# Four chunks of hidden products ahead of the gate matrix, half of its one-hots on DVE, and three PSUM banks with an earlier u in the chunk loop of a PEER block

## The chip, the cores and the metric

The kernel runs on one core of one Trainium2 chip. Its time is that of the device, in microseconds (us), as the median of several runs. The engines are named as in the profile: PE is TensorE, DVE is VectorE, ACT is ScalarE, POOL is GpSimd, SP is SyncE, which here only issues transfers. All arithmetic is fp32; a product of two fp32 matrices is made as three fp32r products of a high and a low half (hi·hi, hi·lo, lo·hi).

## What is computed

One decoder block on 1024 tokens of width 1024 (16 meta tokens are put ahead and dropped at the end): two convolution mixers, a residual sum, and then the PEER channel mixer, in which almost all the time goes. With `h` the residual stream:

```python
hn = rms_norm(h, norm_ffn_g)
q = (hn @ w_q).reshape(tokens, 8, 256)
s1 = einsum("thd,hnd->thn", q[..., :128], sub_keys[:, 0]); s2 = einsum(... q[..., 128:], sub_keys[:, 1])
v1, i1 = top_k(s1, 16); v2, i2 = top_k(s2, 16)
vals, pos = top_k(v1[..., :, None] + v2[..., None, :], 16)   # over the 256 pairs of each head
idx = i1[pos // 16] * 128 + i2[pos % 16]                     # 8 x 16 experts of 16384 for each token
gates = softmax(vals)
act = gelu(einsum("chkd,cd->chk", u[idx], hn))
h = h + einsum("chk,chkd->cd", act * gates, v[idx])
out = rms_norm(h, final_norm_g)
```

`u` and `v` are tables of 16384 rows of 1024 floats, 64 MB each.

## The kernel before

The 1024 tokens are 8 tiles of 128. For the first five tiles (`ND`, 640 tokens) the experts are computed **densely**: all 16384 rows of u and v pass through PE, in 128 chunks of 128 rows, and a gate matrix that is zero except at the chosen experts weighs them. For the last three tiles the chosen rows are **gathered** by 768 indirect transfers (`fetch`, 512 KB each, issued by POOL), and DVE multiplies and adds them.

Stages, in the order of the program:

1. `front`: norms, projections, convolutions, `w_q`, scores, and the top-16 searches, which run on DVE and end the stage.
2. `gate_matrix`: for each of the five tiles, in 16 steps of 8 tokens, DVE makes the one-hot `o2` of the second key (L691), DVE and ACT make the one-hot `o1` of the first key times the gate, and PE multiplies them into a 128x128 gate matrix for each token (L705, 1280 instructions); ACT copies it out of PSUM (`st`, L708), SP stores it (`g_d`). Of the eight one-hots `o1` of a step, the first six come from a comparison in bf16 on DVE (`ob`, L693) that ACT scales (L698), and the last two from DVE alone (L700).
3. `hidden_ahead`, a generator that runs beside stage 2: for the 16 chunks 5, 13, 21, ... (`AHEAD`) it makes gelu(u·hn) early, in the PE time that the gates leave, and stores it (`p_d`). It has 64 steps (16 chunks x 2 halves of the width x 2 segments of 320 tokens, 12 products of 128x320 each). `LEAD = 4` steps are taken ahead of the gates, 0.6 (`RATE`) after each step of 8 tokens, the rest after the last gate.
4. `token_experts` for the three gathered tiles (L545, L549).
5. `dense`: for each chunk `c` a half of u at a time is transposed on PE (`tr`, L733), split by ACT (`uhi`, L154) and DVE (`ulo`, L155), and multiplied into two PSUM banks `mm` (L186 to L188: 24 products a half); ACT takes the gelu out of the banks (`p`, L824), DVE weighs it (L807), ACT and DVE split it (`phi`, `plo`). An AHEAD chunk loads `p` from `p_d` instead. The chunk of v is loaded raw and split (`vhi` on ACT, `vlo` on DVE). Every four chunks (`GRP`) `down` multiplies p and v: ten PSUM banks `ms` of 12 products of 128x512 each, added into `acc` by DVE (L791). Between these stand the gather steps (`advance`; L611 and L637 on DVE). At the end `finish` norms each tile and stores it.

Each engine runs its own instructions in the order in which the program put them; a waiting instruction holds up all behind it on its engine, and a waiting transfer on SP all transfers behind it there. The raw chunks of u and of v share three slots (`raw`, 512 KB each): a chunk of u holds its slot until its second half is transposed, a chunk of v until `vlo` is made. PSUM has 8 banks, and before they are 2 for `tr`, 2 for `mm` and 4 for `ms`, in every stage.

Of the kernel before, what the change touches and what calls it, by code (L numbers as in the profile page):

```python
# [10 lines left out]
F32 = mybir.dt.float32  # L11
F32R = mybir.dt.float32r
# [6 lines left out]
PSUM = bass.MemoryType.PSUM  # L19
DRAM = bass.MemoryType.DRAM  # L20

P = 128
D = 1024
# [19 lines left out]
GB_T = 64  # L43
GB, LAG = 8, 6
AHEAD = list(range(5, NK, 8))
# [4 lines left out]
PACE = (2, 2, 2, 2, 1, 1, 1, 1, 1, 1)  # L50
LEAD = 4
HEAD = 4
# [9 lines left out]
class Block:  # L62
    def __init__(self, ctx, tc, t):
        self.ctx, self.tc, self.nc, self.t = ctx, tc, tc.nc, t
        self.n = 0
        self.last = {}
        self.const = ctx.enter_context(self.pool("const", 1))
        self.small = ctx.enter_context(self.pool("small", 2))
        self.keep = ctx.enter_context(self.pool("keep", 1))
        self.ptr = ctx.enter_context(self.pool("ptr", 2, space=PSUM))  # L70
        self.pmm = ctx.enter_context(self.pool("pmm", 2, space=PSUM))
        self.pms = ctx.enter_context(self.pool("pms", 4, space=PSUM))
        self.dram = ctx.enter_context(self.pool("dram", 1, space=DRAM))

    def pool(self, name, bufs, right=False, **kw):
        self.n += 1
        if "space" not in kw:
            kw["reuse_waits"] = "tile"
        if right:
            kw["side"] = "right"  # L80
        return self.tc.tile_pool(name=f"{name}{self.n}", bufs=bufs, **kw)

    def name(self, s):
# [7 lines left out]
    def constants(self):  # L91
# [3 lines left out]
        self.identb = self.tile(const, [P, P], BF16, "identb")  # L95
        nc.scalar.copy(self.identb, self.ident)
        self.ones = self.tile(const, [P, P], F32, "ones")
        nc.vector.memset(self.ones, 1.0 / C)
# [482 lines left out]

    def gather_constants(self):
        self.gfin = self.tile(self.ga, [P, D], F32, "gfin", bufs=1)
        self.nc.scalar.dma_start(self.gfin, self.t["final_norm_g"].rearrange("(o d) -> o d", o=1).broadcast_to([P, D]))

# [60 lines left out]
    def finish(self, ti, h):  # L646
        o = self.tile(self.ga, [P, D], F32, "row")
        self.row_norms([(o, h, P)], self.gfin, None)
        self.nc.sync.dma_start(self.t["out"][0, ti * P:(ti + 1) * P], o)
# [4 lines left out]
    def gate_matrix(self, first, routes):  # L654

        nc, V = self.nc, self.nc.vector
        W, X, B = 8, 6, GB_T
        with self.pool("gm", 2, right=True) as gm:
# [68 lines left out]
    def prep_u(self, c, q):  # L727

        if q == 0:
            self.raw = self.load("peer_u", c)  # L730
        ps = self.tile(self.ptr, [P, 4, P], F32, "tr")
        for k in range(4):
            self.nc.tensor.transpose(ps[:, k, :], self.raw[:, (4 * q + k) * P:(4 * q + k + 1) * P], self.ident)  # L733
        uT = [self.tile(self.de, [P, 4, P], F32R, "u" + s, bufs=3) for s in ("hi", "lo")]
        self.split(*uT, ps)
        return uT

# [6 lines left out]
    def hidden_ahead(self, pool):  # L744

        T = ND * P
        segs = segments(T)
        uT = self.prep_u(AHEAD[0], 0)
        for i, c in enumerate(AHEAD):
            pu = [self.tile(self.pms, [P, 512], F32, "ms")[:, :s.stop - s.start] for s in segs]  # L750
            for q in range(2):
                cur = uT
                for s, ps in zip(segs, pu):
                    self.hidden(ps, cur, q, s)
                    if q == 1:
                        p = self.tile(pool, [P, segs[0].stop], F32, "pa")[:, :s.stop - s.start]
                        self.nc.scalar.activation(p, ps, AF.Gelu_apprx_tanh)
                        self.nc.sync.dma_start(self.p_d[i, :, s], p)
                    if s is segs[0]:
                        if q == 0:  # L760
                            uT = self.prep_u(c, 1)
                        elif i + 1 < len(AHEAD):
                            uT = self.prep_u(AHEAD[i + 1], 0)
                    yield

    def dense(self, stream):
# [9 lines left out]
        with self.pool("dn", 2, right=True) as dn:  # L776
# [19 lines left out]
            main = [c for c in range(NK) if c not in AHEAD]  # L796
            uT = [self.prep_u(main[0], q) for q in range(2)]
            for c in range(NK):
# [17 lines left out]
                else:  # L816
                    main.pop(0)
                    pu = [self.tile(self.pmm, [P, 512], F32, "mm")[:, :s.stop - s.start] for s in segs]
                    for q in range(2):
                        for s, ps in zip(segs, pu):  # L820
                            self.hidden(ps, uT[q], q, s)
                            if q == 1:
# [3 lines left out]
                                advance(1)  # L826
                        if main:
                            uT[q] = self.prep_u(main[0], q)
                        if q == 0:
# [12 lines left out]
def body(tc, t):  # L842
    with ExitStack() as ctx:
# [11 lines left out]
        b.gb = ctx.enter_context(b.pool("gb", GB))  # L855
        b.gather_constants()
        b.last = {}
# [20 lines left out]
```

## Time and profile before

| | |
|---|---|
| runs | 2879.54, 2871.32, 2884.39 us; median 2879.54 |
| profiled execution | 2871.9 us, span 2870.1 us |
| busy share of the span | PE 94%, DVE 85%, ACT 33%, POOL 32% |
| chain that ended last | PE 64%, DVE 16%, ACT 9%, DMA 9%; of that raw v loads 7%, `o` on ACT (L698) 4% |
| mean TensorE clock granted | 0.987 of full |
| gate loop, first to last L705 | 679.0 to 984.7 us |
| chunk loop | 1027 to 2861 us |

The busy share of PE is an average over stages with different limits: in the top-16 part PE stands, in the gate stage ACT is as full as PE, in the chunk loop PE is fullest. The profiled execution lies 7.6 us under the median of the three runs.

### The profile page before, as it was taken

Reading aid. Unit: us, or ns where it says so; the run is one execution under the profiler, and the core shown is the slowest. Engines: PE = TensorE matmul, PEld = TensorE weight load, DVE = VectorE, ACT = ScalarE, POOL = GpSimd, SP = SyncE. Lnnn points to the kernel's source line nnn. Section 1 sums busy time; section 2 is a strip of 40 time slices with the busy share of each in tenths; the row PEclk is TensorE's granted clock in tenths of the full one; section 3 lists DMA queues with packets and bytes.
Section 4 is the critical chain, followed back from the end, with each engine's and each line's share of the span. In section 5 each row is a group of like instructions: output and inputs, shape, how many; then the busy total and the mean of one; then the engine's idle time right before and its main releaser. Section 6 shows DMA issues by size and latency. Waiting matters only on the chain.

```text
span 2870.1 us, 43789 instructions
## 1 busy us (share of the span) xinstructions
PE 2712.1 (94%) x16481; PEld 2485.9 (87%) x16481; DVE 2434.9 (85%) x5024; ACT 945.3 (33%) x1887; POOL 919.0 (32%) x793
## 2 busy tenths in 40 slices
PE   6999999986999989999999999999999999999998
PEld 6999989976888988898888889888888889888887
DVE  5998777998777569889889898889899988989986
ACT  4112431116999731222222212222222222222222
POOL 0000011110000025445544454445544544545440
PEclk9999999998999999999999999999999999999999
DMA  3112221101656789999989999999999999989992
GB/s 112 45 45 82 95 96 37 38 19 43 181 163 174 211 315 325 329 321 332 324 311 319 320 331 334 321 329 326 333 326 325 326 327 319 326 316 333 330 313 82
DMA packets 299540, 684.08 MB, mean 238 GB/s; under 512 B 20617, under 2 KB 153737, under 8 KB 299328
## 3 DMA queue, kind: packets, MB, share of 16 engines
q0 software_dynamic: 110592, 402.70, 39.4%
q1 hardware_dynamic: 188256, 276.92, 28.9%
q8 instruction: 130, 2.13, 0.3%
q10 hardware_dynamic: 480, 1.65, 0.1%
q14 instruction: 82, 0.67, 0.1%
HBM read 624.05 MB, written 57.15 MB: 237 GB/s over the span
## 4 chain that ended last, share of the span: by engine, by line
PE 64%; DVE 16%; ACT 9%; DMA 9%; issue 2%; SPq 0%; DVEq 0%; ACTq 0%
PE ms L188 12%; PE ms L187 12%; PE ms L186 12%; PE mm L188 7%; PE mm L186 7%; PE mm L187 7%; DMA raw<-in_peer_v_dram 7%; ACT o L698 4%; DVE row L637 3%; PE tr L733 2%; PE mm L705 2%; DVE vlo L155 2%; ACT st L708 2%; DVE g L611 1%; DVE s L467 1%
## 5 line engine op out<-in xcount | busy, mean ns | idle before, releaser
L588 POOL DMA_INDIRECT g<-in_peer_u_dram,ix x384 | 435.1, 1133 | 831.1 <-DVE ix L549 391.1
L186 PE MATMUL mm<-nhi,uhi 128*128 128x320 f32 x1792 | 573.1, 320 | 32.4 <-ACT p L824 32.0
L588 POOL DMA_INDIRECT g<-in_peer_v_dram,ix x384 | 440.6, 1147 | 455.1 <-DVE row L637 387.6
L188 PE MATMUL mm<-nhi,ulo 128*128 128x320 f32 x1792 | 557.7, 312 | 15.7 <-DVE ulo L155 15.1
L187 PE MATMUL mm<-nlo,uhi 128*128 128x320 f32 x1792 | 554.7, 310 | 0.0
L186 PE MATMUL ms<-vhi,phi 128*128 128x512 f32 x1280 | 501.4, 392 | 1.5 <-ACT phi L154 1.4
L188 PE MATMUL ms<-vhi,plo 128*128 128x512 f32 x1280 | 498.8, 390 | 0.0
L187 PE MATMUL ms<-vlo,phi 128*128 128x512 f32 x1280 | 498.7, 390 | 0.0
L637 DVE SCALAR_TENSOR_TENSOR row<-g,w,row 128x1024 f32<-128x1024 f32 x384 | 492.0, 1281 | 6.1 <-DMA row<-hd 4.7
L611 DVE SCALAR_TENSOR_TENSOR g<-g,row 128x1024 f32<-128x1024 f32 x384 | 464.5, 1222 | 0.0
L186 PEld LDWEIGHTS mm<-nhi,uhi 128*128 128x128 f32 x1792 | 338.4, 189 | 42.4 <-ACT p L824 40.3
L188 PEld LDWEIGHTS mm<-nhi,ulo 128*128 128x128 f32 x1792 | 337.5, 188 | 24.9 <-DVE ulo L155 23.9
L187 PEld LDWEIGHTS mm<-nlo,uhi 128*128 128x128 f32 x1792 | 338.7, 189 | 1.2
L154 ACT CAST phi<-p 128x320 fp32r<-128x320 f32 x256 | 116.4, 459 | 561.6 <-PE ms L187 340.8
L186 PEld LDWEIGHTS ms<-vhi,phi 128*128 128x128 f32 x1280 | 240.5, 188 | 51.0 <-ACT phi L154 2.4
L188 PEld LDWEIGHTS ms<-vhi,plo 128*128 128x128 f32 x1280 | 240.5, 188 | 50.6 <-DVE plo L155 0.5
L154 ACT CAST vhi<-raw 128x1024 fp32r<-128x1024 f32 x128 | 132.9, 1049 | 456.7 <-PE ms L188 316.5
L187 PEld LDWEIGHTS ms<-vlo,phi 128*128 128x128 f32 x1280 | 240.6, 188 | 49.0
L791 DVE TENSOR_TENSOR acc<-acc,ms 128x512 f32<-128x512 f32 x320 | 219.4, 685 | 34.7 <-PE ms L188 33.9
L155 DVE TENSOR_TENSOR ulo<-tr,uhi 128x512 fp32r<-128x512 f32 x256 | 175.4, 687 | 52.7 <-ACT uhi L154 51.8
L155 POOL TENSOR_TENSOR wlo<-wraw,whi 128x1024 fp32r<-128x1024 f32 x16 | 38.0, 2378 | 568.6 <-ACT whi L154 568.6
L154 ACT CAST uhi<-tr 128x512 fp32r<-128x512 f32 x256 | 149.4, 584 | 198.3 <-PE tr L733 195.9
(201 smaller groups left out, 4978.5 us busy)
## 6 DMA issues: line engine op xcount, KB each, us to landing
raw<-in_peer_u_dram SPq DMA_DIRECT2D x128, 512.0 KB
raw<-in_peer_v_dram SPq DMA_DIRECT2D x128, 512.0 KB
gd<-st SPq DMA_DIRECT2D x40, 1024.0 KB
g<-gd SPq DMA_DIRECT2D x64, 640.0 KB
wraw<-in_w_in_dram SPq DMA_DIRECT2D x20, 512.0 KB
wraw<-in_peer_w_q_dram SPq DMA_DIRECT2D x16, 512.0 KB
g<-in_peer_u_dram,ix POOLq DMA_INDIRECT x384
g<-in_peer_v_dram,ix POOLq DMA_INDIRECT x384
```

What stands on the lines that cost most here:

```text
L154: nc.scalar.copy(hi, src)
L155: self.mark(eng.tensor_tensor(lo, src, hi.bitcast(F32), op=OP.subtract))
L186: self.nc.tensor.matmul(ps, lh(a), rh(b), start=first and i == 0, stop=False)
L187: self.nc.tensor.matmul(ps, lh(a), rl(b), start=False, stop=False)
L188: last = self.nc.tensor.matmul(ps, ll(a), rh(b), start=False, stop=final and i == n - 1)
L588: self.nc.gpsimd.indirect_dma_start(out=g, out_offset=None, in_=self.t[table][0], in_offset=bass.IndirectOffsetOnAxis(ap=ix, axis=0))
L611: self.after(nc.vector.scalar_tensor_tensor(ut, ut, 1.0, b["x"], op0=OP.mult, op1=OP.mult, accum_out=b["act"][:, k:k + 1]))
L637: self.after(nc.vector.scalar_tensor_tensor(b["h"], b.pop(k), res[0][:, k:k + 1], b["h"], op0=OP.mult, op1=OP.add))
L698: nc.scalar.activation(o1[:, m, :], ob[:, :, m], AF.Copy, scale=eT[:, 2, c:c + 1])
L705: nc.tensor.matmul(pg[:, :, m], o2[:, 4 * z + m, :], o1[:, 4 * z + m, :], start=True, stop=True)
L708: nc.scalar.copy(st[:, :, c:c + 4], pg)
L791: self.mark(V.tensor_tensor(acc[:, i, dd], acc[:, i, dd], po, op=OP.add))
```

## The change

Five edits in one. (a) `LEAD` goes from 4 to 16: four AHEAD chunks ahead of the gates instead of one, so that with 48 steps beside the gates all 64 are used up and none stands behind them. (b) `X` goes from 6 to 4: of each step's eight one-hots four are made on ACT and four on DVE, and `ob` shrinks from 128x768 to 128x512. (c) In `hidden_ahead` the low half of u no longer comes from a subtraction on DVE: PE adds minus `uhi` into the bank that holds the transposes (one 128x512 product with a negative identity, L760), and ACT copies the rest out (L761). (d) `banks` makes the PSUM pools anew ahead of `dense`, with 2 banks for `tr`, 3 for `mm` and 3 for `ms`. (e) In `dense` u is transposed and split three halves ahead instead of two, with four buffers instead of three, and the raw chunk of u is loaded right after the last half of the one ahead (`early`). `finish` loads `final_norm_g` (512 KB) for each tile into a gather slot instead of keeping it.

```diff
-LEAD = 4
+LEAD = 16
...
-        W, X, B = 8, 6, GB_T
+        W, X, B = 8, 4, GB_T
...
+    def banks(self, tr, mm, ms):
+
+        if self.psum is not None:
+            self.psum.close()
+        self.psum = ExitStack()
+        mk = lambda name, bufs: self.psum.enter_context(
+            self.tc.tile_pool(name=self.name(name), bufs=bufs, space=PSUM, reuse_waits="tile"))
+        self.ptr, self.pmm, self.pms = mk("ptr", tr), mk("pmm", mm), mk("pms", ms)
...
     def finish(self, ti, h):
         o = self.tile(self.ga, [P, D], F32, "row")
-        self.row_norms([(o, h, P)], self.gfin, None)
+        g = self.tile(self.gb, [P, D], F32, "g")
+        self.nc.sync.dma_start(g, self.t["final_norm_g"].rearrange("(o d) -> o d", o=1).broadcast_to([P, D]))
+        self.row_norms([(o, h, P)], g, None)
...
     def prep_u(self, c, q):
 
         if q == 0:
-            self.raw = self.load("peer_u", c)
+            self.raw = self.early.pop(c, None) or self.load("peer_u", c)
...
+    def prep_ahead(self, c, q):
...
+        for k in range(4):
+            nc.tensor.matmul(ps[:, k, :], self.raw[:, (4 * q + k) * P:(4 * q + k + 1) * P], self.ident,
+                             is_transpose=True, start=k == 0, stop=k == 3)
+        hi, lo = (self.tile(self.de, [P, 4, P], F32R, "u" + s, bufs=4) for s in ("hi", "lo"))
+        flat = lambda x: x.rearrange("p a b -> p (a b)")
+        nc.scalar.copy(hi, ps)
+        nc.tensor.matmul(flat(ps), self.minus, flat(hi), start=False, stop=True, skip_group_check=True)
+        nc.scalar.copy(lo, ps)
+        return hi, lo
...
-            uT = [self.prep_u(main[0], q) for q in range(2)]
+            parts = [(c, q) for c in main for q in range(2)]
+            made = []
+
+            def prepare():
+
+                if parts:
+                    c, q = parts.pop(0)
+                    made.append(self.prep_u(c, q))
+                    if q == 1 and parts:
+                        self.early[parts[0][0]] = self.load("peer_u", parts[0][0])
+
+            for _ in range(3):
+                prepare()
...
                     for q in range(2):
+                        uT = made.pop(0)
                         for s, ps in zip(segs, pu):
-                            self.hidden(ps, uT[q], q, s)
+                            self.hidden(ps, uT, q, s)
...
-                        if main:
-                            uT[q] = self.prep_u(main[0], q)
+                        prepare()
...
+        b.banks(2, 3, 3)
```

How the built order moves, at three places. (The lines of the changed kernel are some ten higher: L186 to L188 are L197 to L199 there, L154 is L165, L676 is L686, L705 is L715, L724 is L734, L824 is L862.)

PE, at the point where the gates begin (L676 and L686 turn the first tile's key lists; `ms` is a bank, `n` the normed tokens). Before:

```order
L449 MATMUL ms_6564<-kT_2909,qT_6562 128x128 x3
L733 MATMUL tr_6635<-ident_75,raw_6633 128x128 x4
L733 MATMUL tr_6658<-ident_75,raw_6633 128x128 x4
L186 MATMUL ms_6644<-nhi_110,uhi_6640 128x320
L187 MATMUL ms_6644<-nlo_111,uhi_6640 128x320
L186 MATMUL ms_6645<-nhi_110,uhi_6640 128x320
L187 MATMUL ms_6645<-nlo_111,uhi_6640 128x320
L676 LDWEIGHTS oh_6426
L676 MATMUL ms_6348<-identb_80,oh_6426 128x128
```

After, the last of the rows that stand ahead of it:

```order
L197 MATMUL ms_6882<-nhi_112,uhi_6900 128x320
L198 MATMUL ms_6882<-nlo_113,uhi_6900 128x320
L760 MATMUL tr_6934<-uhi_6939,minus_82 128x512
L199 MATMUL ms_6882<-nhi_112,ulo_6901 128x320
L197 MATMUL ms_6882<-nhi_112,uhi_6900 128x320
L198 MATMUL ms_6882<-nlo_113,uhi_6900 128x320
L199 MATMUL ms_6882<-nhi_112,ulo_6901 128x320
L197 MATMUL ms_6882<-nhi_112,uhi_6900 128x320
L198 MATMUL ms_6882<-nlo_113,uhi_6900 128x320
L199 MATMUL ms_6882<-nhi_112,ulo_6901 128x320
L686 LDWEIGHTS oh_6428
L686 MATMUL ms_6350<-identb_80,oh_6428 128x128
```

Ahead of the first gate row PE has 192 products of 128x320 now (four chunks of 48), where it had 4 of the first chunk; a product on PE does not pass another, so the gates wait for all of them.

PE, behind the last gate product. Before (140 more products of 128x320 and 19 transposes follow, and then L545):

```order
L705 MATMUL mm_9984<-o_1509_9972,o_1508_9971 128x128
L705 MATMUL mm_9990<-o_1509_9972,o_1508_9971 128x128 x4
L187 MATMUL ms_10015<-nlo_111,uhi_9967 128x320
L188 MATMUL ms_10015<-nhi_110,ulo_9968 128x320
L186 MATMUL ms_10015<-nhi_110,uhi_9967 128x320
L187 MATMUL ms_10015<-nlo_111,uhi_9967 128x320
L188 MATMUL ms_10015<-nhi_110,ulo_9968 128x320
```

After:

```order
L715 MATMUL mm_10235<-o_1539_10223,o_1538_10222 128x128
L198 MATMUL ms_10097<-nlo_113,uhi_10115 128x320
L715 MATMUL mm_10241<-o_1539_10223,o_1538_10222 128x128
L199 MATMUL ms_10097<-nhi_112,ulo_10116 128x320
L715 MATMUL mm_10241<-o_1539_10223,o_1538_10222 128x128 x3
L556 LDWEIGHTS identb_80
L556 MATMUL mm_10303<-oh_10291,identb_80 128x128
```

Nothing of the 16 chunks is left there, and the rows of `token_experts` (L556, before L545) follow at once.

ACT in the chunk loop, behind the `down` of chunks 8 to 11. Chunk 13 is an AHEAD chunk, so the next chunks with products of u are 14, 15 and 16; the pairs `mm_12312`, `mm_12313` and before `mm_12257`, `mm_12258` are the banks of chunk 14, `mm_12409` and `mm_12354` the first bank of chunk 15. Raw 12403 and 12348 are v of chunk 14, raw 12500 and 12445 v of chunk 15. Before:

```order
L154 CAST vhi_12226<-raw_12228 128x1024 [waits DMAHW5_49,PE_49]
L154 CAST phi_12232<-p_12239 128x320 [waits DMAHW2_49,DVE_49]
L154 CAST vhi_12247<-raw_12249 128x1024 [waits DMAHW6_49,PE_49]
L154 CAST uhi_12290<-tr_12285 128x512 [waits PE_49]
L154 CAST vhi_12346<-raw_12348 128x1024 [waits DMAHW4_49]
L824 ACTIVATE p_12309<-mm_12257 128x320 [waits DVE_49,PE_49]
L154 CAST phi_12255<-p_12309 128x320 [waits DVE_49]
L824 ACTIVATE p_12329<-mm_12258 128x320 [waits PE_49]
L154 CAST uhi_12342<-tr_12337 128x512 [waits PE_49]
L154 CAST phi_12255<-p_12329 128x320 [waits DVE_49]
L154 CAST vhi_12443<-raw_12445 128x1024 [waits DMAHW6_49]
L154 CAST uhi_12387<-tr_12382 128x512 [waits PE_49]
```

After:

```order
L165 CAST vhi_12302<-raw_12304 128x1024 [waits DMAHW7_49,PE_49]
L165 CAST uhi_12343<-tr_12338 128x512 [waits PE_49]
L862 ACTIVATE p_12364<-mm_12312 128x320 [waits DVE_49,PE_49]
L165 CAST vhi_12401<-raw_12403 128x1024 [waits DMAHW4_49]
L165 CAST phi_12310<-p_12364 128x320 [waits DVE_49]
L862 ACTIVATE p_12384<-mm_12313 128x320 [waits PE_49]
L165 CAST uhi_12397<-tr_12392 128x512 [waits PE_49]
L165 CAST phi_12310<-p_12384 128x320 [waits DVE_49]
L165 CAST uhi_12440<-tr_12435 128x512 [waits PE_49]
L165 CAST vhi_12498<-raw_12500 128x1024 [waits DMAHW6_49]
L862 ACTIVATE p_12461<-mm_12409 128x320 [waits PE_49]
L862 ACTIVATE p_12481<-mm_12410 128x320 [waits DVE_49,PE_49]
```

The first gelu of chunk 14 now stands ahead of `vhi` of chunk 14 and no longer behind it; `vhi` of chunk 15 still stands ahead of the first gelu of chunk 15.

SP at the same place, the raw loads of v 14, u 16, v 15, u 17 before:

```order
L724 DMA raw_12348<-in_peer_v_dram 128x1024 [waits DMAHW5_49,DVE_49]
L724 DMA raw_12380<-in_peer_u_dram 128x1024 [waits DMAHW6_49,DVE_49]
L724 DMA raw_12445<-in_peer_v_dram 128x1024 [waits DMAHW1_49,PE_49]
L724 DMA raw_12479<-in_peer_u_dram 128x1024 [waits DMAHW4_49,DMAHW7_49,DVE_49,Activation_49]
L724 DMA raw_12726<-in_peer_v_dram 128x1024 [waits DMAHW6_49,DMAHW0_49,DVE_49]
```

After, u 16, v 14, u 17, v 15, u 18:

```order
L734 DMA raw_12347<-in_peer_u_dram 128x1024 [waits DMAHW5_49,DVE_49]
L734 DMA raw_12403<-in_peer_v_dram 128x1024 [waits DMAHW4_49,PE_49]
L734 DMA raw_12444<-in_peer_u_dram 128x1024 [waits DMAHW7_49,DVE_49]
L734 DMA raw_12500<-in_peer_v_dram 128x1024 [waits DMAHW6_49,DMAHW4_49,DVE_49]
L734 DMA raw_12543<-in_peer_u_dram 128x1024 [waits DMAHW3_49,PE_49]
```

A load that waits for DVE takes the slot of a v, one that waits for PE that of a u. By the addresses in the two built programs, u 16 takes the slot of v 13 before and of v 12 after; v 14 that of v 12 before, and after that of u 15, so behind the transposes of its second half; v 15 that of u 15 before, and after that of v 14. From there on the changed kernel has two slots under u and one under v: v 15, v 16, v 17, v 18, v 19 and v 20 follow each other through the same slot.

## Rows read from the trace of the kernel before

**Rows 1.** Windows: us, each engine's busy time, TensorE clock, DMA share, GB/s

```profile
700.00:950.00 250.00, 232.89 (x1739) 210.75 (x1738) 188.56 (x371) 245.66 (x595) 0.00 (x0) 0.99 0.60 170
1050.00:2800.00 1750.00, 1697.37 (x9632) 1533.33 (x9631) 1565.17 (x2294) 435.03 (x809) 867.20 (x760) 1.00 0.91 324
```

**Rows 2.** Timeline of PE ahead of the gates: start, us, instruction, [idle before <-releaser]

```profile
...
663.70 3.50 PE L676 MATMUL ms<-identb,oh 128*128 128x128 bf16 x32 [14.24 <-DVE s L467]
...
672.96 0.47 PE L186 MATMUL ms<-nhi,uhi 128*128 128x320 f32 x1
673.23 0.47 PE L187 MATMUL ms<-nlo,uhi 128*128 128x320 f32 x1
...
679.00 0.38 PE L705 MATMUL mm<-o,o 128*128 128x128 f32 x2
```

**Rows 3.** Instruction groups of the gate loop (675:985): busy, mean ns | idle before

```profile
...
L698 ACT ACTIVATE o<-ob,eT 128x128 f32<-128x128 bf16 x480 | 186.2, 470 | 2.4 <-DVE ob L693 2.2
...
L708 ACT COPY st<-mm 128x512 f32<-128x512 f32 x160 | 91.0, 583 | 3.9 <-PE mm L705 3.4
...
L700 DVE TENSOR_SCALAR o<-iota,eT 128x128 f32<-128x128 f32 x160 | 47.8, 343 | 0.0
L693 DVE TENSOR_TENSOR ob<-iob,e1b 128x768 bf16<-128x768 bf16 x80 | 42.5, 556 | 41.6 <-ACT o L698 41.4 <-ACT e1b L684 0.2
...
L155 DVE TENSOR_TENSOR ulo<-tr,uhi 128x512 fp32r<-128x512 f32 x25 | 17.2, 686 | 2.2 <-ACT uhi L154 2.1
```

**Rows 4.** Timeline of PE after the last gate product

```profile
...
985.67 0.49 PE L733 MATMUL tr<-ident,raw 128*128 128x128 f32 x3
...
1008.13 1.07 PE L545 MATMUL mm<-oh,identb 128*128 128x128 bf16 x16
```

**Rows 5.** Instruction groups of the chunks (1050:2800)

```profile
L186 PE MATMUL mm<-nhi,uhi 128*128 128x320 f32 x1712 | 547.7, 320 | 32.4 <-ACT p L824 32.0 <-issue 0.3
L188 PE MATMUL mm<-nhi,ulo 128*128 128x320 f32 x1713 | 533.1, 312 | 15.7 <-DVE ulo L155 15.1
...
L154 ACT CAST vhi<-raw 128x1024 fp32r<-128x1024 f32 x120 | 124.5, 1049 | 442.6 <-PE ms L188 316.5 <-DMA raw<-in_peer_v_dram 126.1
```

**Rows 6.** Timeline of SP after the output products of chunks 8 to 11

```profile
1210.53 0.33 SPq L724 DMA_DIRECT2D raw<-in_peer_v_dram  x1
...
1217.76 0.33 SPq L724 DMA_DIRECT2D raw<-in_peer_v_dram  x1
1219.91 0.33 SPq L724 DMA_DIRECT2D raw<-in_peer_u_dram  x1
```

**Rows 7.** Timeline of ACT there

```profile
...
1216.80 1.05 ACT L154 CAST vhi<-raw 128x1024 fp32r<-128x1024 f32 x1 [2.41 <-DMA raw<-in_peer_v_dram]
1217.75 0.43 ACT L824 ACTIVATE p<-mm 128x320 f32<-128x320 f32 x1
...
1224.87 1.05 ACT L154 CAST vhi<-raw 128x1024 fp32r<-128x1024 f32 x1 [2.59 <-DMA raw<-in_peer_v_dram]
```

**Rows 8.** Timeline of PE there

```profile
...
1213.17 0.60 PE L733 MATMUL tr<-ident,raw 128*128 128x128 f32 x4
...
1217.13 0.60 PE L733 MATMUL tr<-ident,raw 128*128 128x128 f32 x4
1218.23 0.42 PE L186 MATMUL mm<-nhi,uhi 128*128 128x320 f32 x1 [0.50 <-ACT p L824]
```

**Rows 9.** Timeline of SP after the output products of chunks 12 to 15

```profile
...
1266.19 0.33 SPq L724 DMA_DIRECT2D raw<-in_peer_v_dram  x1
...
1273.27 0.33 SPq L724 DMA_DIRECT2D raw<-in_peer_v_dram  x1
```

**Rows 10.** Timeline of ACT there

```profile
...
1270.93 1.05 ACT L154 CAST vhi<-raw 128x1024 fp32r<-128x1024 f32 x1 [1.77 <-DMA raw<-in_peer_v_dram]
...
1277.53 1.06 ACT L154 CAST vhi<-raw 128x1024 fp32r<-128x1024 f32 x1 [1.37 <-DMA raw<-in_peer_v_dram]
```

**Rows 11.** Window of a later group, just after PE had waited for ACT

```profile
...
1622.50:1625.50 3.00, 3.00 (x15) 2.96 (x14) 3.00 (x5) 1.24 (x3) 0.94 (x1) 0.54 0.76 214
```

## What was predicted

> **What bounds the kernel now.** I read the windows first, then for each stage the groups of instructions with their idle time, and at last the timelines of the places where an engine waits. In the gate stage the windows show ACT busy 245.66 of 250 us and PE 232.89, DVE 188.56 [rows 1]: both PE and ACT are nearly full, ACT the fuller. In the chunk loop PE is busy 1697.37 of 1750 us, DVE 1565.17, ACT 435.03, the DMA engines 0.91 at 324 GB/s [rows 1]: PE bounds it, with DVE and DMA close behind. What can still be taken from PE there is its idle time: 32.0 us for the gelu `p` on ACT and 15.1 us for `ulo` on DVE [rows 5], 47.1 us in all. In each case PE's bank or operand is late because ACT stands at `vhi`, which waits 126.1 us in the stretch for a raw v [rows 5]. That is the thing to follow: the gelu is cheap, but it stands in line behind a load.
>
> **The start of the gates (LEAD).** Before, PE starts on the key lists (L676) at 663.70, where it had idled 14.24 us for DVE's scores; the first gate product is at 679.00 [rows 2]. After, four chunks stand ahead on PE. A half chunk (24 products, four transposes) takes 1217.13 − 1213.17 = 3.96 us at full clock [rows 8], so four chunks take 31.7 us. They begin where that idle time does, at 663.70 − 14.24 = 649.5, but the banks for the second chunk are those of the scores, which DVE gives back at about 664 and 672, where PE goes on before [rows 2]. So about one chunk fits into the wait, and three, 23.8 us, come after 668: L686 at about 692, later by 28, less what DVE finishes meanwhile: before, 15.3 us lie between L676 and the first gate product because DVE is still at the top-16; with DVE done that shrinks to some 8. I put the first gate product at 700, 21 us later. Bounds: 15 (half of the second chunk fits too) and 28 (the clock stays at its lower level longer: at 672.96 and 673.23 products start 0.27 us apart [rows 2]).
>
> **The gate loop (LEAD, X, the low half on PE).** It takes 984.7 − 679.0 = 306 us. At the shares of [rows 1] ACT has 300 us of work in it, PE 285, DVE 230. ACT loses two of six one-hots, 160 x 186.2/480 = 62 us, and gains a copy of 583 ns for each of 22 low halves, 13 us [rows 3]: 251. DVE gains 160 one-hots at 47.8/160 = 0.30, 48 us, loses a third of `ob`, 14, and the 25 `ulo`, 17 [rows 3]: 247. PE has 44 products fewer (551 for 595 in the built order) and 22 of 128x512 more, at most 0.26 us each (3.96/24 x 512/320 [rows 8]): 285 − 7 + 6 = 284, which counts modelled ends twice at times; by the starts it is nearer 280. So PE is the bound after. ACT now is 98% full in its loop; if PE reaches the same, the loop takes 288 us, 18 less. Bounds: 0 (three engines each above 80% wait for each other in turn) and 26 (PE without a gap).
>
> **Behind the gates.** From 985.67 to 1008.13 PE does the rest of the AHEAD chunks [rows 4]. None is left: 22.5 us, no bound needed, except that L545 could find DVE's lists not ready; DVE has slack there, and I put nothing.
> Gate stage: 18 + 22.5 − 21 = about **20 us won**; bounds −5 and 33.
>
> **The chunk loop.** Three banks remove the case in which one late gelu stops PE at once, and u three halves ahead the waits for `ulo`: at most 47.1 us. Giving one bank from `ms` to `mm` I cost at nothing: DVE's addition follows 12 products of 128x512, and three banks leave PE two such spans, 2 x 12 x 0.26 = 6 us, before it needs the bank again; if DVE were later, it would be 1 to 2 us for each `down`.
> But the raw slots go the other way. In the built order two of three are under u and one under v, so the v of the next chunk is loaded only after `vlo` of the last. From the rows: a load takes 6.27 us (1210.53 to 1216.80), 7.11 (1217.76 to 1224.87) [rows 6, 7], 4.74 and 4.26 [rows 9, 10]; from `vhi`'s start to the next load that its slot lets go 3.11 (1216.80 to 1219.91) or 2.34 (1270.93 to 1273.27) [rows 6, 7, 9, 10]. One round of a v slot so takes 6.6 to 10.2 us, and PE needs one v for each 7.92 us.
> I follow it for both kinds of group, with T the end of the last `down`, 1209.65 (1213.17 less 24 products).
> (i) AHEAD group (three chunks of u, 14, 15, 16). v 14 is loaded when u 15 is transposed, T+4.3, lands T+10.5 to 11.4; v 15 at T+12.9 to 14.5, lands T+17.1 to 21.6; then 1.05 for `vhi` and 0.43 for the gelu of chunk 15, which stands behind it on ACT: T+18.6 to 23.1. PE wants that bank, with three banks, for the second segment of chunk 16, at T+15.9+1.8 = T+17.7. It waits 0.9 to 5.4 us. I take 1.6, near the low end, because the second loads of a group (4.26) come when DVE has waited and asked for fewer gathers.
> (ii) Full group (17 to 20). v 17 is loaded at T+0.9, v 18 and v 19 one round each later; the gelus are due at T+9.7, T+17.7 and T+25.7 and come at T+9.2 to 10.1, 15.8 to 20.3, 22.5 to 30.5: 0 to 4.8 us, I take 0.4.
> Before, the same two places cost 47.1 us over the 15.4 pairs of groups in the stretch, 3.1 us a pair (0.50 us in this AHEAD group [rows 8]). After, 2.0 a pair, 31 us. Won: **16 us**; bounds 33 won (0.9 a pair) and 110 lost (10.2 a pair, every load at its longest).
> `finish` now loads `final_norm_g`; the two loads inside the loop stand on SP ahead of raw loads and wait for a gather slot, of which one comes free each 1750/760 = 2.3 us [rows 1]: **2 us lost**, bounds 0 and 5. The six at the end are issued ahead of the last norms.
>
> **Sum.** 2871.9 − 20 − 16 + 2 = 2838 us, against the profiled execution (span 2870.1 and 1.8 around it). That execution lies 7.6 us under the median 2879.54; against the median the same sum is 2845. I keep 2838.
>
> **A rule that speaks against it.** Just after a PE wait in a later group the granted clock is 0.54 of full for 3 us, which is the lower level of 1.2 GHz, though the stretch as a whole has 1.00 [rows 1, 11].
> By the Trainium skill, "TensorE: Matmul & The Clock Gate", section "HAM oscillation — how this bites in real kernels", a loop that waits for a transfer on each pass falls back to the lower clock each time and pays for the restart on each pass. Were it so here, waits that stay once or twice in each of the 30 groups would cost 1.4 us more each (0.46 of 3 us), some 43 us, and the time would be 2881; the mean of 1.00 in the stretch says that the trace seldom shows it.
>
> **The rivals.**
> *One slot for v (slower).* ACT's order puts `vhi` of chunk 15, 18, 19 ahead of the gelus that free the banks. If a load takes 7 us under full DMA and `vlo` comes 3 us after, the round is 10 us against 7.92, the lag adds up through the group, and PE loses 5.4 + 4.8 us a pair. Above 5.4 us a pair (rounds of about 9 us) it eats the gate stage's gain as well: 2871.9 − 20 + 2 + 15.4 x (5.4 − 3.1) = 2889 at 5.4 + 0, past 2900 with both. For it: 7.11 and 6.27 are rows, DMA stands at 0.91. Against it: 4.26 and 4.74 are rows too, and a waiting DVE asks for fewer gathers.
> *The chunk loop stays as it is.* v's lateness takes what the banks give: 2871.9 − 20 + 2 = 2854.
> *The gate start eats the gate stage.* Start 28 us later, loop 9 shorter: 22.5 + 9 − 28 = 4 won; with 16 − 2 of the chunk loop 2854.
> *All waits go.* Loads near 4.3 us: 2871.9 − 20 − 33 + 2 = 2821, and 2808 with the gate stage at its best.
> *The restart at the lower clock after each wait*: 2881, as above.
>
> **How the numbers follow.** Forecast (gate stage and chunk loop both win, 2818 to 2850) 0.46; all waits go (2800 to 2818) 0.08; chunk loop unchanged (2850 to 2865) 0.16; gate start late 0.08; one slot for v, net loss in the loop (2865 to 2910) 0.18; restart 0.04. A measurement of this kernel can tell about 0.5%, 14 us. Faster holds the first two, most of the next two: 0.67; same 0.18; slower 0.15. The range 2800 to 2884 leaves out the worse half of the v case and the best ends; the likeliest case alone is 2818 to 2850.
>
> **What would show it.** First gate product near 700, last near 988, L545 straight after; ACT under 88% and PE near full in the loop. In the chunk loop: PE's idle for `p` under 25 us and for `ulo` under 8; raw v loads issued one `vlo` after the other; ACT's `vhi` waiting for raw v more than 126.1 us. If PE waits for `p` more than 60 us, the v slot is the cause and the forecast is wrong; if the first gate product is past 708, the start is.

## The result and the profile after

The changed kernel takes 2844.08 us (median of 4 runs, 2841.62 to 2848.59), the kernel before 2877.38 beside it: a ratio of 0.9881, 95% interval 0.986 to 0.9902, so 33 us less. Forecast were 2838 us and a gain both in the gate stage and in the chunk loop. The time came out, the sum did not: the gate stage won more than twice what was put down, and the chunk loop lost.

The profiled execution is the longest of the four, 2848.59 us, span 2846.8. Its windows, as [rows 1] (after the stretch and its length: busy us and count of PE, of PE's weight loads, of DVE, ACT and POOL, then clock, DMA share and GB/s):

```profile
700.00:950.00 250.00, 245.62 (x1949) 233.93 (x1948) 223.73 (x531) 223.04 (x547) 0.00 (x0) 1.00 0.63 180
1050.00:2800.00 1750.00, 1688.63 (x9542) 1525.63 (x9541) 1540.88 (x2258) 419.20 (x801) 878.51 (x743) 0.99 0.90 321
```

In the gate stage PE has gone from 232.89 to 245.62 of 250 us, ACT from 245.66 to 223.04, DVE from 188.56 to 223.73: PE bounds it now. In the chunk loop PE is less busy than before, 1688.63 for 1697.37. The timeline of PE, as [rows 2, 4, 8]:

```profile
691.50 1.96 PE L686 MATMUL ms<-identb,oh 128*128 128x128 bf16 x32
...
698.22 0.94 PE L715 MATMUL mm<-o,o 128*128 128x128 f32 x6
...
964.33 1.95 PE L556 MATMUL mm<-oh,identb 128*128 128x128 bf16 x32
...
1179.47 0.63 PE L743 MATMUL tr<-ident,raw 128*128 128x128 f32 x4 [1.16 <-DMA raw<-in_peer_u_dram]
...
1190.95 0.41 PE L197 MATMUL mm<-nhi,uhi 128*128 128x320 f32 x1 [1.17 <-ACT p L862]
```

L686 at 691.50 and the first gate product at 698.22 are what was forecast (692 and 700). `token_experts` begins at 964.33, where it began at 1008.13: 43.8 us earlier, against 20. From there to the end of the span it is 1882.5 us now and was 1862.0: 20.5 us given back in this execution. The groups of the gate loop (705:980), as [rows 3]:

```profile
L708 ACT ACTIVATE o<-ob,eT 128x128 f32<-128x128 bf16 x305 | 103.3, 409 | 1.9 <-PE mm L715 1.7 <-DVE ob L703 0.2
...
L718 ACT COPY st<-mm 128x512 f32<-128x512 f32 x156 | 88.7, 587 | 17.2 <-PE mm L715 16.9
L710 DVE TENSOR_SCALAR o<-iota,eT 128x128 f32<-128x128 f32 x308 | 84.3, 343 | 0.0
...
L703 DVE TENSOR_TENSOR ob<-iob,e1b 128x512 bf16<-128x512 bf16 x76 | 29.9, 421 | 0.7 <-ACT o L708 0.6
```

`ob` used to wait 41.4 us for ACT's one-hots and now waits 0.6, and it is ACT that waits for PE, 16.9 us at `st`. The groups of the chunk loop (1050:2800), as [rows 5]:

```profile
L197 PE MATMUL mm<-nhi,uhi 128*128 128x320 f32 x1688 | 543.2, 322 | 17.3 <-ACT p L862 17.0
...
L199 PE MATMUL mm<-nhi,ulo 128*128 128x320 f32 x1688 | 524.8, 311 | 0.0
...
L743 PE MATMUL tr<-ident,raw 128*128 128x128 f32 x840 | 130.1, 278 | 44.0 <-DMA raw<-in_peer_u_dram 25.8 <-DVE ulo L166 15.2 <-DVE vlo L166 2.6
L165 ACT CAST vhi<-raw 128x1024 fp32r<-128x1024 f32 x122 | 128.2, 1051 | 599.5 <-PE ms L199 302.9 <-DMA raw<-in_peer_v_dram 287.3 <-PE tr L743 8.9
```

PE's wait for the gelu fell from 32.0 to 17.0 us and that for `ulo` ahead of a product from 15.1 to nothing. But the transposes (L743), which waited 3.0 us in all before, now wait 25.8 us for a raw u and 15.2 for `ulo` to give back one of the two `tr` banks. And ACT waits 287.3 us for a raw v, where it was 126.1. SP and ACT behind the `down` of chunks 8 to 11, as [rows 6, 7]; first SP:

```profile
1172.41 0.33 SPq L734 DMA_DIRECT2D raw<-in_peer_u_dram  x1
1174.82 0.33 SPq L734 DMA_DIRECT2D raw<-in_peer_v_dram  x1
...
1184.27 0.33 SPq L734 DMA_DIRECT2D raw<-in_peer_v_dram  x1
```

then ACT:

```profile
1181.93 1.05 ACT L165 CAST vhi<-raw 128x1024 fp32r<-128x1024 f32 x1 [4.91 <-DMA raw<-in_peer_v_dram]
...
1189.52 1.04 ACT L165 CAST vhi<-raw 128x1024 fp32r<-128x1024 f32 x1 [2.34 <-DMA raw<-in_peer_v_dram]
1190.47 0.76 ACT L862 ACTIVATE p<-mm 128x320 f32<-128x320 f32 x2
```

The round of the one v slot can be read off: v 14 asked for at 1174.82, cut from 1181.93, v 15 asked for at 1184.27, cut from 1189.52, and only then, at 1190.47, the gelu of chunk 15, for which PE waits 1.17 us at 1190.95. The raw u asked for at 1172.41 lands 7 us later too, 1.16 us after PE wants it.

### The profile page after: what moved, and what is told of

Its sections match the earlier page's. It is cut to its first block, busy times and chain, and to the rows that moved or that the text cites. A ratio compares the mean times of both kernels' runs of the same rounds, so it can differ in the third digit from the quotient of the medians.

```text
span 2846.8 us, 44008 instructions
## 1 busy us (share of the span) xinstructions
PE 2707.5 (95%) x16513; PEld 2494.9 (88%) x16513; DVE 2434.5 (86%) x5152; ACT 881.6 (31%) x1762; POOL 950.9 (33%) x793
## 4 chain that ended last, share of the span: by engine, by line
PE 48%; DVE 27%; DMA 14%; issue 6%; ACT 4%; SPq 0%; ACTq 0%; DVEq 0%
DMA raw<-in_peer_v_dram 11%; PE ms L198 10%; PE ms L197 10%; PE ms L199 10%; DVE row L645 6%; DVE g L619 6%; PE mm L715 4%; PE mm L197 4%; PE mm L198 4%; PE mm L199 4%; DVE ulo L166 2%; DVE vlo L166 2%; DVE acc L817 2%; DVE p L845 1%; DVE plo L166 1%
## 5 line engine op out<-in xcount | busy, mean ns | idle before, releaser
L596 POOL DMA_INDIRECT g<-in_peer_u_dram,ix x384 | 449.3, 1170 | 790.0 <-DVE g L619 368.9
L596 POOL DMA_INDIRECT g<-in_peer_v_dram,ix x384 | 459.6, 1197 | 442.2 <-DVE row L645 366.4
L197 PE MATMUL mm<-nhi,uhi 128*128 128x320 f32 x1792 | 577.1, 322 | 18.0 <-ACT p L862 17.0
L199 PE MATMUL mm<-nhi,ulo 128*128 128x320 f32 x1792 | 557.8, 311 | 0.0
L197 PE MATMUL ms<-vhi,phi 128*128 128x512 f32 x1280 | 502.0, 392 | 0.1
L199 PE MATMUL ms<-vhi,plo 128*128 128x512 f32 x1280 | 498.8, 390 | 0.0
L197 PEld LDWEIGHTS mm<-nhi,uhi 128*128 128x128 f32 x1792 | 341.5, 191 | 26.2 <-ACT p L862 24.1
L199 PEld LDWEIGHTS mm<-nhi,ulo 128*128 128x128 f32 x1792 | 340.2, 190 | 0.0
L165 ACT CAST vhi<-raw 128x1024 fp32r<-128x1024 f32 x128 | 134.4, 1050 | 617.1 <-DMA raw<-in_peer_v_dram 304.9
L166 DVE TENSOR_TENSOR vlo<-raw,vhi 128x1024 fp32r<-128x1024 f32 x128 | 156.7, 1224 | 167.8 <-ACT vhi L165 167.6
L165 ACT CAST phi<-p 128x320 fp32r<-128x320 f32 x256 | 115.8, 460 | 594.7 <-PE ms L198 312.0
L199 PEld LDWEIGHTS ms<-vhi,plo 128*128 128x128 f32 x1280 | 240.6, 188 | 50.7
L197 PEld LDWEIGHTS ms<-vhi,phi 128*128 128x128 f32 x1280 | 240.7, 188 | 50.3 <-DVE acc L817 1.4
L743 PE MATMUL tr<-ident,raw 128*128 128x128 f32 x896 | 139.5, 280 | 53.8 <-DMA raw<-in_peer_u_dram 31.6
```

The lines of the kernel that those rows point to most:

```text
L165: nc.scalar.copy(hi, src)
L166: self.mark(eng.tensor_tensor(lo, src, hi.bitcast(F32), op=OP.subtract))
L197: self.nc.tensor.matmul(ps, lh(a), rh(b), start=first and i == 0, stop=False)
L199: last = self.nc.tensor.matmul(ps, ll(a), rh(b), start=False, stop=final and i == n - 1)
L596: self.nc.gpsimd.indirect_dma_start(out=g, out_offset=None, in_=self.t[table][0], in_offset=bass.IndirectOffsetOnAxis(ap=ix, axis=0))
```

## The experiments

Twelve kernels, in three sets, each timed beside the kernel before.

**First set: the two parts of the change, and the two parts of the chunk loop's.** `gates_alone` is the changed kernel with the chunk loop's banks and order of u put back; the other two put back one of them, and `gates_raw4` adds a slot:

```diff
             for _ in range(3):       # gates_alone, banks_two_ahead, gates_raw4: range(2)
                 prepare()
...
-                    if q == 1 and parts:          # left out in the same three
-                        self.early[parts[0][0]] = self.load("peer_u", parts[0][0])
...
-        b.banks(2, 3, 3)             # left out in gates_alone, three_ahead_alone, gates_raw4
...
-        r = self.tile(self.de, [P, D], F32, "raw", bufs=3)
+        r = self.tile(self.de, [P, D], F32, "raw", bufs=4)      # gates_raw4
```

Expected of `gates_alone`: 

> The changed kernel's edits up to the last gate stay; in the chunk loop PSUM is 2, 2, 4 banks again and u is prepared two halves ahead with its raw load in front of its own transposes, as before. Theory A (the chunk loop's part of the change loses time, because two raw slots stand under u and one under v): the first down starts as early as in the changed kernel (about 1031 us) and from there to the end it takes 1793 us as before, not 1807; about 2830 us, 14 less than the changed kernel. Theory B (the loop lost nothing by itself, and only shifted because DMA and gathers start differently): as the changed kernel, 2844.

Expected of `banks_two_ahead`: 

> The changed kernel with 2, 3, 3 banks, but u two halves ahead and no early raw load. Theory A: the third bank takes most of PE's 32.0 us of waits for the gelu away and the slots are those of before; PE waits for p under 15 us, ACT waits for raw v about 126 us as before; 2805 to 2820 us. Theory C (three ms banks or the bank order cost the time): no better than the changed kernel, 2844, with gates_alone faster than it.

Expected of `three_ahead_alone`: 

> The changed kernel with 2, 2, 4 banks in the loop, u three halves ahead and raw u loaded early. Theory A: the one slot for v makes the gelus late and two banks pass it on to PE at once; PE waits for p over 40 us, ACT for raw v near 290 us; 2860 to 2880. Theory C: faster than the changed kernel, 2830.

Expected of `gates_raw4`: 

> As gates_alone, with a fourth raw slot (and three buffers for the halves of u). Theory A: v no longer waits for a slot; ACT's wait for raw v falls from 126 us to under 50 and PE's for p from 32 to under 15; 2810 us. Theory D (a raw v is late because the DMA engines are full, not for want of a slot): the waits stay, 2830.

| kernel | median us | ratio to before (95%) |
|---|---|---|
| changed | 2844.08 | 0.9881 (0.986 to 0.9902) |
| gates_alone | 2833.41 | 0.9849 (0.9832 to 0.9865) |
| banks_two_ahead | 2842.29 | 0.9886 (0.9866 to 0.9906) |
| three_ahead_alone | 2861.64 | 0.994 (0.9921 to 0.9959) |
| gates_raw4 | 2831.96 | 0.9842 (0.9823 to 0.9862) |

Without the chunk loop's part the kernel is 10.7 us faster than with it, as theory A said. (The two intervals overlap a little, but the four runs, 2832.82 to 2834.79, all lie under the four of the changed kernel, with the kernel before at 2877 beside both.) Three halves ahead with an early load, by itself, loses 28 us. But the third bank, which by theory A should have won 10 to 25, won nothing (its four runs spread from 2832.17 to 2848.74; the trace is of the fastest, and why the others are longer was not traced). The waits say why (1050:2780; us in all, times, longest), first those of `gates_alone`:

```profile
ACT vhi L165 <- DMA raw<-in_peer_v_dram: 127.2, 56, 6.9
...
PE mm L197 <- ACT p L860: 29.1, 29, 2.8
...
PE mm L199 <- DVE ulo L166: 13.5, 20, 3.0
...
PE tr L743 <- DMA raw<-in_peer_u_dram: 3.5, 7, 0.9
```

and those of `banks_two_ahead`:

```profile
ACT vhi L165 <- DMA raw<-in_peer_v_dram: 125.3, 57, 5.9
...
PE mm L199 <- DVE ulo L166: 33.1, 37, 2.1
...
PE tr L743 <- DMA raw<-in_peer_u_dram: 9.3, 11, 1.7
...
PE mm L197 <- ACT uhi L165: 7.1, 6, 2.6
...
PE mm L197 <- ACT p L860: 1.0, 2, 0.7
```

The wait for the gelu is gone, 1.0 us, and what ACT does next after the same late `vhi`, `uhi` and with it `ulo`, is what PE waits for now: 51 us in all for 46 in `gates_alone`. The time is also the one that theory C named, but PE has no wait for the addition that frees an `ms` bank here, and `three_ahead_alone`, for which C expected 2830, took 2861.64. Beside the early u the third bank is worth something: 2861.64 without it, 2844.08 with it. With only two banks and u three halves ahead, the gelu takes it all (`three_ahead_alone`, the same window):

```profile
ACT vhi L165 <- DMA raw<-in_peer_v_dram: 253.7, 65, 8.7
...
PE mm L197 <- ACT p L862: 56.2, 36, 3.6
...
PE tr L743 <- DMA raw<-in_peer_u_dram: 17.4, 14, 2.4
```

A fourth raw slot beside the old order of u moved nothing either (`gates_raw4`, the same window):

```profile
ACT vhi L165 <- DMA raw<-in_peer_v_dram: 157.6, 44, 7.9
...
PE mm L197 <- ACT p L860: 26.9, 18, 4.9
PE mm L199 <- DVE ulo L166: 22.8, 30, 1.2
```

Theory A, as a matter of slots alone, fell here: ACT still stands at `vhi` for 157.6 us, in the order that the program's scheduler gave it. No run gave a fourth slot to the changed kernel's own order, with u three halves ahead.

**Second set: is it ACT's order, and what is X worth?** `late_cut` takes `gates_raw4`, asks for v at the same place, but cuts it one chunk later and on ACT behind that chunk's first gelu. `half_gathers` is `gates_alone` with every second gathered row left out. `gates_x6` and `gates_lead4` put one number back.

```diff
-                vh, vl = (self.tile(dn, [P, D], F32R, "v" + s, bufs=GRP) for s in ("hi", "lo"))
-                self.split(vh, vl, self.load("peer_v", c))
-                pend.append((ph, pl, vh, vl))
+                pend.append([ph, pl, self.load("peer_v", c)])     # late_cut
...
+            def cut():               # called after the next chunk's products, ahead of down
+                if pend and len(pend[-1]) == 3:
+                    raw = pend[-1].pop()
+                    vh, vl = (self.tile(dn, [P, D], F32R, "v" + s, bufs=GRP) for s in ("hi", "lo"))
+                    self.after(nc.scalar.copy(vh, raw))           # after the marked gelu
+                    self.mark(V.tensor_tensor(vl, raw, vh.bitcast(F32), op=OP.subtract))
+                    pend[-1] += [vh, vl]
...
-                                nc.scalar.activation(p, ps, AF.Gelu_apprx_tanh)
+                                ins = nc.scalar.activation(p, ps, AF.Gelu_apprx_tanh)
+                                if s is segs[0]:
+                                    self.mark(ins)
...
-        W, X, B = 8, 4, GB_T
+        W, X, B = 8, 6, GB_T         # gates_x6
-LEAD = 16
+LEAD = 4                             # gates_lead4
...
-                b[k] = self.fetch("peer_v", r[1][:, k:k + 1])
+                b[k] = self.fetch("peer_v", r[1][:, k:k + 1]) if k % 2 == 0 else b[k - 1]   # half_gathers; peer_u too
```

Expected of `late_cut`: 

> gates_alone with four raw slots, three buffers for the halves of u, and the cut of v (vhi, vlo) one chunk later and on ACT behind the next chunk's first gelu, so that no gelu stands behind a raw v that has just been asked for. Theory A (the waits of PE come from ACT standing at vhi for a late raw v): ACT's wait for raw v falls from 127 us to under 20, PE's for p, ulo and raw u from 46 in all to under 15; about 2800 us. Theory D (DVE or the DMA engines bound the loop, and a wait taken away at one place comes back at another): PE's waits only change their names; 2822 to 2835.

Expected of `half_gathers`: 

> gates_alone with every second gather left out (the gathered row before is used again, so the last three tiles come out otherwise); DVE's and POOL's other work stays. Theory A and D both say that a raw chunk lands sooner with less traffic: DMA share from 0.91 to about 0.6, landing of raw v from 6.5 us to near 3.5, ACT's wait for raw v under 40 us. If PE's waits fall under 15 us and the time to about 2800, the landing time is what the waits are made of; if PE still waits over 30 us, DVE's order is.

Expected of `gates_x6`: 

> gates_alone with six one-hots on ACT again. By the prediction's sum ACT gets 62 us of work back and bounds the loop: 266 us become about 315, 2875 to 2885 us. Rival (X was worth little, LEAD and the low half on PE did it): under 2845.

Expected of `gates_lead4`: 

> gates_alone with LEAD = 4. The first gate product comes some 19 us earlier (679), the loop stays at 266 us, and 22 us of products stand behind the last gate again: about 2836 us, a difference of 3. Rival (the wait for the scores hides most of the four chunks): 2845 to 2850.

`late_cut` takes 2779.81 us, ratio 0.9668 (0.9651 to 0.9684): 53.6 us less than `gates_alone` and 52.2 less than `gates_raw4`, which has the same slots; more than was expected. Its groups (1050:2700):

```profile
L197 PE MATMUL mm<-nhi,uhi 128*128 128x320 f32 x1680 | 534.8, 318 | 0.0
L199 PE MATMUL mm<-nhi,ulo 128*128 128x320 f32 x1680 | 519.8, 310 | 3.5 <-DVE ulo L166 3.4
...
L743 PE MATMUL tr<-ident,raw 128*128 128x128 f32 x840 | 126.4, 273 | 8.6 <-DMA raw<-in_peer_u_dram 8.3
...
L826 ACT CAST vhi<-raw 128x1024 fp32r<-128x1024 f32 x120 | 125.1, 1042 | 0.0
```

`vhi` does not wait at all, PE 12 us. On the timeline of ACT the cast now stands behind the gelu, and the raw v has landed (in 1050:2700 a cast starts a median of 34.6 us after SP asked for its v):

```profile
1169.69 0.44 ACT L868 ACTIVATE p<-mm 128x320 f32<-128x320 f32 x1 [1.17 <-PE mm L199]
1170.03 1.04 ACT L826 CAST vhi<-raw 128x1024 fp32r<-128x1024 f32 x1
```

The edit moves `vlo` on DVE with the cast; what that does by itself was not separated. Theory D, that DVE or the DMA engines would bring the waits back elsewhere, fell: both do the same work in less time (DVE is busy 1531.62 of 1650 us for 1474.42 in `gates_alone`, the DMA share is 0.93 for 0.92). `half_gathers` takes 2770.67 us (two executions), 0.9632 (0.9611 to 0.9652), with the DMA share down to 0.67:

```profile
ACT vhi L165 <- DMA raw<-in_peer_v_dram: 57.3, 53, 3.0
...
PE mm L197 <- ACT p L862: 4.3, 8, 1.1
...
PE mm L199 <- DVE ulo L166: 1.5, 1, 1.5
```

ACT still waits 57.3 us for raw v, more than the 40 expected, but PE only 5.8 in its products. From SP's issue to the cast of a raw v that ACT had to wait for it is a median of 4.6 us, and 6.4 in `gates_alone`. So the late landing is the one half of the cause, and ACT's order the other; less traffic, or the new order together with a fourth slot, each takes PE's waits away. (`half_gathers` also halves what POOL issues, so the landing time is not changed alone in it.)

The gate loop, first and last of the 1280 gate products (one row each: lengths min/median/max in ns, first and last start), for `gates_x6`, 2876.54 us, 0.9992 (0.9977 to 1.0008):

```profile
L715 PE MATMUL mm<-o,o x1280: 270/275/582, 699.7 to 1006.0; 128*128 128x128 f32 x183
```

and for `gates_lead4`, 2829.4 us, 0.9841 (0.9823 to 0.9858):

```profile
L715 PE MATMUL mm<-o,o x1280: 270/275/377, 685.3 to 941.4; 128*128 128x128 f32 x183
```

With six one-hots on ACT the loop takes 306 us again and the whole gain is gone: X carries it. LEAD is worth nothing: the loop starts and ends earlier with LEAD = 4 (the first gate product at 685.3 where 679 was expected, the loop 256 us long where 266 was), and the products left over then fill the 27 us from 941.4 to `token_experts` at 968.0; the time is if anything shorter than that of `gates_alone`.

**Third set.** `late_cut_raw3` is `late_cut` with three raw slots, `late_cut_233` has 2, 3, 3 banks, `late_cut_lead4` LEAD = 4; `before_x4` is the kernel before with X = 4 and nothing else. The edits are lines shown above.

Expected of `late_cut_raw3`: 

> late_cut with three raw slots again. Theory A1 (ACT's order behind a late v is the cause by itself): 2780 to 2790, ACT's wait for raw v still under 20 us. Theory A2 (order and slots together: a v that is cut a chunk later holds its slot a chunk longer, so that raw u comes late): PE waits for raw u over 30 us, 2810 to 2835.

Expected of `late_cut_233`: 

> late_cut with the changed kernel's 2, 3, 3 banks. If the third bank only covered gelus that stood behind a late v, there is nothing left for it: 2775 to 2785. If it has a worth of its own, under 2770; if three ms banks are too few once PE does not wait, over 2790.

Expected of `late_cut_lead4`: 

> late_cut with LEAD = 4. As in gates_lead4 the products only move from ahead of the gates to behind them: 2772 to 2782.

Expected of `before_x4`: 

> The kernel before with nothing but X = 4. If X is the whole gain of the gate stage, as gates_x6 says, the loop falls from 306 to about 270 us and the time to 2835 to 2842. Rival (X only pays with the low half of u on PE, because DVE is full otherwise): 2850 to 2865.

| kernel | median us | ratio to before (95%) |
|---|---|---|
| late_cut_raw3 | 2951.74 | 1.0264 (1.0245 to 1.0283) |
| late_cut_233 | 2776.55 | 0.9654 (0.9635 to 0.9673) |
| late_cut_lead4 | 2776.05 | 0.9657 (0.9638 to 0.9675) |
| before_x4 | 2844.24 | 0.9888 (0.9869 to 0.9908) |

The late cut needs its fourth slot. With three, a v holds its slot a chunk longer and the raw u comes late, worse than A2 had it (1050:2700):

```profile
L743 PE MATMUL tr<-ident,raw 128*128 128x128 f32 x752 | 118.5, 282 | 123.8 <-DMA raw<-in_peer_u_dram 123.8
```

The third bank has nothing left to cover, and LEAD moves nothing here either. `late_cut`, `late_cut_233` and `late_cut_lead4` are not told apart by their intervals; each beats both kernels, by 97 to 100 and by 64 to 68 us. And `before_x4` by itself is as fast as the whole change, 2844.24 for 2844.08.

## Why the prediction was right, and where it was not

**The time** came out near by luck. In the profiled executions the gate stage ended 43.8 us earlier where 20 were put down, and the rest took 20.5 us longer where 14 less were put down (16 won in the chunk loop, 2 lost in `finish`): two misses of some 24 and 35 us in opposite directions. The likeliest case, in which both stages win, did not come. What came is the mechanism of the rival with one slot for v beside a gate stage that won more than any bound allowed. The 2 us for `finish` were not measured apart.

**The start of the gates** held: 692 and 691.50 for L686, 700 and 698.22 for the first gate product.

**The gate loop** is the first term that was mis-sized. It was put at 288 us with PE as the bound and took 266 (698.2 to 964.2). The term of 18 us came to 40. That PE would bound it was right (98% busy); the prices for ACT and DVE, 251 and 247, were a little high (at the windows' shares 223.04/250 and 223.73/250 of 266 they come to 237 and 238, so that ACT stands at 89%, just above the 88% named as a sign). The floor of 280 to 284 for PE was wrong: it took PE's busy share before, 93%, as work. `before_x4` shows that it is not. Its gate loop has the same 2113 PE instructions as that of the kernel before; first the kernel before, then `before_x4`:

```profile
679.00:984.90 305.90, 285.54 (x2113) 259.40 (x2112) 231.47 (x465) 300.43 (x730) 0.00 (x0) 0.99 0.56 159
...
682.40:954.00 271.60, 264.94 (x2113) 253.00 (x2112) 256.72 (x625) 230.11 (x567) 0.00 (x0) 1.00 0.63 179
```

For the same instructions PE counts as busy for 285.54 us when ACT feeds it late, and for 264.94 when it is fed in time. The gate products of the two kernels, in the same windows:

```profile
L705 PE MATMUL mm<-o,o 128*128 128x128 f32 x1280 | 194.4, 292 | 20.3 <-ACT o L698 10.8 <-ACT st L708 8.2
...
L705 PE MATMUL mm<-o,o 128*128 128x128 f32 x1280 | 178.2, 282 | 5.3 <-ACT st L708 2.8 <-ACT o L698 2.2
```

A product lasts 292 ns on the mean, but 1280 of them keep PE busy for 194.4 us, 152 ns for each, because they overlap; fed in time they overlap more, and it is 139 ns for each. The clock, 0.99 and 1.00, can be 3 of the 20.6 us. The busy time of the weight loads moved far less, from 259.40 to 253.00. The forecast's best case, 26 us less "without a gap", was 280; the loop went below the assumed floor. One small term was too low: the 22 products of the low half (L760) keep PE busy for 10.4 us, 0.47 each, where at most 0.26 was taken.

**Which edit wins it** was put down to all three together, and the text priced LEAD's two sides at 22.5 won and 21 lost, so nearly nothing: that held (`gates_lead4`). X alone won 32 us (`before_x4` against the 2876.34 beside it), which is as much as the whole change. The low half on PE seems to pay only once X is 4: from the first gate product to `token_experts` it is 282.7 us in `gates_lead4` and 295.1 in `before_x4` (682.4 to 977.5), where DVE is fuller (226.85 of 240 us in 700:940, for 221.33). The two kernels differ in a few smaller things too, so this is not shown by an edit of its own. With X = 6 the low half gives ACT more to do, and `gates_x6` wins nothing.

**The chunk loop** was put at 16 us won and lost 10.7 (`gates_alone` against the changed kernel), inside the stated bounds but of the other sign. The chain of the one v slot, worked out ahead as a rival, is what the timelines show: rounds of 9.45 us (1174.82 to 1184.27) and a gelu 1.17 us late in the group shown, for 1.6 taken. Its sum of 31 us for `p` was even too high; 17.0 was measured. What the sum left out is that the same edit makes two other things late: u three halves ahead wants its raw chunk earlier than a slot is free (25.8 us for raw u), and it wants a third `tr` bank, so that the wait for `ulo` of 15.1 us was not removed but moved from the product to the transposes (15.2 us). In all PE stands 61 us in 1050:2800, for 53 before. Of the signs named beforehand, ACT's wait for raw v above 126.1 us came (287.3). That the slot is the cause was not tested by a run that gives this order a fourth one.

**The third bank** was taken as covering a late gelu. It does, and with u two halves ahead it is worth nothing while `uhi` stands in the same line behind the same `vhi`: `banks_two_ahead`. The step that failed is that the two waits of [rows 5] were added up as two costs that can be removed one by one; they are one cost, ACT's stop at `vhi`, seen at two places; with that stop gone (`late_cut`) both waits go, and the third bank adds nothing (`late_cut_233`).

**The restart at the lower clock** (rival, 0.04) did not come as 43 us more in the changed kernel. It is there in smaller size: over 1050:2700 the mean granted clock is 0.992 for 0.998 before, some 10 us.

`gates_alone` is the better kernel of the two halves, and `late_cut` the one that takes the loop's waits away. That `late_cut` won 53.6 us where PE's waits fell only from 45 to 12 can be followed for the most part. In 1050:2700 it puts 3.5% more columns (320 for a product of 128x320) through PE than `gates_alone`, which at the rate of `gates_alone` is 58 us of work. The waits are 33 of these. The other 25 or so lie in the products themselves: PE is busy 0.471 ns for a column in `gates_alone` and 0.464 in `late_cut`. A part of that is overlap lost at each wait: a product of 320 columns lasts 309 ns, and the next one starts 147 ns after it when nothing is late, so each wait costs an estimated 0.16 us that does not count as idle, 54 times in `gates_alone` and 7 times in `late_cut`, 8 us. Another 8 us would be the clock (0.993 and 0.998 in this window); but the pair with LEAD = 4 wins as much, 53.4 us, with 0.999 in both. The rest was not traced.

## What to carry to other kernels

Waits of a fast engine for different operands can be one stop of a slower in-order engine; find the instruction that the slower engine stands at, and move that, before giving the fast one more buffers. When an instruction on that engine waits for a transfer, put it behind the work that others wait for, and give the transfer a slot for the longer time: the order alone, without the slot, was the worst kernel here. And the busy time of PE while it is fed late is no floor for its time when it is fed well.

## What the runs showed of the hardware

A wait on PE can cost more than its length. In the kernel before, the granted clock was 0.54 of full for 3 us from 1622.50 [rows 11], about 1 us after this wait:

```profile
1621.36 0.41 PE L186 MATMUL mm<-nhi,uhi 128*128 128x320 f32 x1 [2.21 <-ACT p L824]
```

Where such waits are many it shows in the whole loop; first `late_cut`, in which PE waits 12 us, then `late_cut_raw3`, in which it waits 127:

```profile
1050.00:2700.00 1650.00, 1637.98 (x9410) 1495.22 (x9409) 1531.62 (x2225) 433.47 (x793) 827.84 (x740) 1.00 0.93 337
...
1050.00:2700.00 1650.00, 1523.33 (x8509) 1378.47 (x8508) 1392.26 (x2060) 389.65 (x713) 753.90 (x675) 0.98 0.87 306
```

With one decimal more the clock is 0.998 and 0.979, which makes some 31 us beside 115 us more of waits, and `three_ahead_alone` with 68 us lies between, at 0.987. With fewer waits the clock does not follow them: the kernels with 45 to 50 us of waits range from 0.993 (`gates_alone`) to 0.999 (`gates_lead4`). The Trainium skill, "TensorE: Matmul & The Clock Gate", section "HAM oscillation — how this bites in real kernels", says that a loop whose matmuls wait for transfers falls back to the lower clock and pays for it on each pass; the trace agrees in part: in `late_cut_raw3` PE waits 70 times, mostly for a raw u, and the clock is lower in 25 of the 165 stretches of 10 us in this window.
